# Half of the ktile pairs of the second MLP products by seven block products in place of eight

## The chip, the cores and the metric

The kernel runs on one core of one Trainium2 chip. The metric is the device time of one launch in microseconds (us). Engines are named as the profile names them: PE is TensorE, DVE is VectorE, ACT is ScalarE, POOL is GpSimd, and SP issues DMAs. PEld is TensorE's loading of stationary tiles.

## The reference

A trunk of two layers on an input of 256 tokens by 2048, in float32. Each layer has a mixer (layer 0: compressed, selected and window attention beside a low-rank one; layer 1: three dilated attentions) and an MLP with a hidden width of 8192:

```
def sq_relu_mlp(h, w1, w2):
    return jnp.square(jax.nn.relu(h @ w1)) @ w2
...
    for layer in range(DEPTH):
        u = rms_norm(h, g_mix_pre)
        m = even_mixer(u, *even_mix) if layer % 2 == 0 else odd_mixer(u, *odd_mix)
        h = h + rms_norm(m, g_mix_post)
        f = sq_relu_mlp(rms_norm(h, g_ffn_pre), *ffns[layer])
        h = h + rms_norm(f, g_ffn_post)
```

The change is in the product with `w2` (8192 by 2048), the second product of the MLP.

## The kernel before

All large products have float32 accuracy out of a reduced matmul format: each operand is split into a high part (`hi`, a rounded copy that ACT writes, `split` in L242 or, with a gain, L245) and a low part (`lo`, the remainder, that DVE writes, L243 or L246). A product is three matmuls: hi by hi, hi by lo, lo by hi. So each weight tile of 128 rows (a "ktile") by 1024 columns, which a 1 MB DMA brings as half of a `raw` tile, costs ACT and DVE one instruction each before PE can use it.

`weights` loads `raw` tiles from a pool of three buffers of their own (`wraw`), and splits them into `whi` and `wlo`, five buffers each. `job` runs a product with the tokens on the output's partitions; `job_T` runs one with the output transposed. A job takes all its ktiles one after another; each of the eight PSUM banks holds one output block, and when the last ktile is done the blocks are evacuated.

The MLP (`mlp`) walks the hidden width in four blocks of 2048 (`FBLK`). Per block:
- ff1, two halves of 1024 hidden columns (in the first block the first half is split in two jobs of 512): `job_T` leaves eight banks, four pairs of them. `done` adds the two parts of a bank (ACT copy L398, DVE add L399); `relu2` squares (ACT L628, L629); `hT.put` splits the result into the stationary tiles `hT` (ACT L242, DVE L243). The banks of the last two ktiles finish one after another.
- ff2, two halves of 1024 output columns: `job` over 16 ktiles, four blocks of 512 columns (2 token tiles by 2 column tiles): 12 matmuls of 512 columns per ktile. The result is copied to (first block, ACT) or added to (later blocks, DVE, L672) the sum `m` in SBUF.

The code is written job after job; the order of each engine's queue is set when the program is built. A load and a split stand as far forward in the queues as their buffers allow, so with pools of their own the first weights of the next job are split ahead of the evacuation of the one that runs. Each engine works through its queue in that order.

The pool `big` (tag "A", 11 buffers of 8 KB per partition) holds `uT`, `hT` (four buffers each), `m`, and the attention's tiles. `s2` is a pool of six scratch tiles of 512 columns. `h`, the residual, has a buffer of its own.

Of the kernel before, what the change touches and what calls it, by code (L numbers as in the profile page):

```python
# [18 lines left out]
P = 128  # L19
# [18 lines left out]
NA, NW = 11, 5  # L38
# [43 lines left out]
def trunk(ctx: ExitStack, tc: tile.TileContext, a: dict, out: bass.AP):  # L82
# [3 lines left out]
    wraw = ctx.enter_context(tc.tile_pool(name="wraw", bufs=3))  # L86
# [86 lines left out]
    h = cst.tile([P, T, D], F, name="h")  # L173
# [122 lines left out]
    def weights(W, k0, nk, cols, gT=None, g0=0, apart=False):  # L296
# [3 lines left out]
        for i in range(0, nk, m0):  # L300
            raw = wraw.tile([P, 2, 1024], F, name="raw")
# [166 lines left out]

    def chunks512(c0, n=1024):
# [101 lines left out]
    class PostNorm:  # L571


        def __init__(self, gname, eps=None):
            self.m = [A([P, D], F, "m") for _ in range(T)]
# [15 lines left out]
        def finish(self, t, then):  # L591
# [28 lines left out]
    def mlp(uT, w1, w2, gT, g0, ss, gname, then):  # L620
# [4 lines left out]
        pn = None  # L625
# [6 lines left out]
        def ff1(b, hT):  # L632
# [19 lines left out]
        eps = []  # L652
        for b in range(nb):
            hT = Split("hT", nk)
            ff1(b, hT)
            if b == 0:
# [5 lines left out]
                pn = PostNorm(gname, eps)  # L662
            end = b == nb - 1
# [554 lines left out]
```

## Time and profile before

| what | us |
|---|---|
| median of 3 runs | 2281.84 (2281.67 to 2282.22) |
| the profiled execution | 2280.53 |
| its span | 2278.6 |
| PE busy | 2255.6 |
| DVE busy | 1346.2 |
| ACT busy | 1250.0 |
| ff2, one half of one block (there are 16) | 87.2 |
| ff1, one half of one block | 88.9 |

The profiled execution has about 1.9 us outside its span. The MLP of layer 0 stands at 348.8 to 1061.7 us of the span, that of layer 1 at 1556.6 to 2267.0 us.

### The profile page before, as it was taken

The numbers are of one execution on the slowest core, as the hardware profiler recorded it, in microseconds if no ns is written. First come the engines' busy times: TensorE is split into PE (matmuls) and PEld (weight loads), VectorE is DVE, ScalarE is ACT, GpSimd is POOL, SyncE is SP. The second block draws the span as 40 slices with busy tenths as digits, with TensorE's granted clock in tenths as the row PEclk, the third lists the DMA queues.
The fourth block names the chain that finished last, engine by engine and source line by source line (L and its number), as shares of the span: only waits on it lengthen the run. The fifth ranks groups of instructions, "written<-read, shape, count | busy, mean of one in ns | idle before, by whom it ended". The sixth has DMA issues, their size and how long they took to land.

```text
span 2278.6 us, 30208 instructions
## 1 busy us (share of the span) xinstructions
PE 2255.6 (99%) x11949; PEld 1937.5 (85%) x11949; DVE 1346.2 (59%) x2059; ACT 1250.0 (55%) x1940; POOL 51.9 (2%) x44
## 2 busy tenths in 40 slices
PE   9999999999999999999999999999999999999997
PEld 9889887888888888887888888887888888888886
DVE  5877547544654554566565677847554554554555
ACT  5766547544644544555556666657554554554553
POOL 0000010000000000011000000001000000000002
PEclk9999999999999999999999999999999999999999
DMA  7844455565465555554554554555565555555553
GB/s 249 247 148 139 140 174 166 198 208 186 168 220 185 185 203 185 185 198 160 188 193 149 184 174 159 178 174 163 192 212 188 188 198 189 186 198 190 185 202 112
DMA packets 131177, 418.58 MB, mean 184 GB/s; under 512 B 6870, under 2 KB 7644, under 8 KB 130524
## 3 DMA queue, kind: packets, MB, share of 16 engines
q1 hardware_dynamic: 131036, 416.66, 54.3%
q8 instruction: 93, 1.52, 0.3%
q14 instruction: 48, 0.39, 0.1%
HBM read 414.54 MB, written 2.10 MB: 183 GB/s over the span
## 4 chain that ended last, share of the span: by engine, by line
PE 90%; issue 5%; DVE 2%; POOL 1%; ACT 1%; DMA 0%; DVEq 0%; POOLq 0%; SPq 0%; ACTq 0%
PE mm L361 27%; PE mm L405 19%; PE mm L409 10%; PE sb L361 6%; PE tb L361 6%; PE tb L405 4%; PE sb L405 4%; PE sb L409 2%; PE tb L409 2%; PE mm L435 2%; PE sb L539 2%; PE mm L443 2%; PE tb L283 1%; DVE h L603 1%; POOL m L589 1%
## 5 line engine op out<-in xcount | busy, mean ns | idle before, releaser
L246 DVE SCALAR_TENSOR_TENSOR wlo<-raw,gT,whi 128x512 fp32r<-128x512 f32 (+4 forms) x621 | 606.6, 1010 | 433.5 <-PE tb L409 208.2
L245 ACT ACTIVATE whi<-raw,gT 128x512 fp32r<-128x512 f32 (+4 forms) x621 | 551.2, 928 | 452.3 <-PE tb L405 238.0
L243 DVE TENSOR_TENSOR wlo<-raw,whi 128x1024 fp32r<-128x1024 f32 x304 | 376.6, 1245 | 356.8 <-ACT whi L242 356.8
L242 ACT ACTIVATE whi<-raw 128x1024 fp32r<-128x1024 f32 x304 | 320.7, 1061 | 384.5 <-PE mm L361 212.3
L405 PE MATMUL mm<-uT,whi 128*128 128x512 f32 x1952 | 503.5, 394 | 0.3 <-ACT z L845 0.3
L405 PEld LDWEIGHTS mm<-uT,whi 128*128 128x128 f32 x1952 | 346.9, 189 | 58.4 <-DVE s L399 0.7
L409 PEld LDWEIGHTS mm<-uT,wlo 128*128 128x128 f32 x1952 | 271.2, 190 | 22.3
L409 PE MATMUL mm<-uT,wlo 128*128 128x256 f32 x1952 | 280.3, 283 | 0.0
L361 PE MATMUL mm<-whi,hT 128*128 128x512 f32 x1024 | 280.3, 389 | 0.0
L361 PEld LDWEIGHTS mm<-whi,hT 128*128 128x128 f32 x1024 | 192.3, 188 | 39.7
L361 PE MATMUL mm<-whi,uT 128*128 128x512 f32 (+1 forms) x640 | 197.0, 398 | 0.0
L361 PE MATMUL mm<-wlo,hT 128*128 128x512 f32 x512 | 162.9, 389 | 0.0
L361 PE MATMUL tb<-whi,hT 128*128 128x512 f32 x512 | 160.6, 390 | 0.0
L361 PE MATMUL sb<-whi,hT 128*128 128x512 f32 x512 | 160.3, 389 | 0.0
L361 PEld LDWEIGHTS mm<-whi,uT 128*128 128x128 f32 x640 | 116.0, 189 | 19.9 <-ACT uT L242 0.2
L405 PE MATMUL tb<-uT,whi 128*128 128x512 f32 x448 | 122.8, 390 | 0.0
L405 PE MATMUL sb<-uT,whi 128*128 128x512 f32 x448 | 122.4, 390 | 0.0
L361 PEld LDWEIGHTS sb<-whi,hT 128*128 128x128 f32 x512 | 96.1, 188 | 20.0
L361 PEld LDWEIGHTS tb<-whi,hT 128*128 128x128 f32 x512 | 96.0, 188 | 19.8
L361 PEld LDWEIGHTS mm<-wlo,hT 128*128 128x128 f32 x512 | 96.2, 188 | 19.6
L361 PE MATMUL mm<-wlo,uT 128*128 128x512 f32 x320 | 104.9, 385 | 0.3 <-DVE wlo L246 0.3
L405 PEld LDWEIGHTS sb<-uT,whi 128*128 128x128 f32 x448 | 82.1, 188 | 15.3
(269 smaller groups left out, 2516.9 us busy)
## 6 DMA issues: line engine op xcount, KB each, us to landing
raw<-in_l_w_ff_dram SPq DMA_DIRECT2D x256, 1024.0 KB, 5.0
raw<-in_l_w_in_dram SPq DMA_DIRECT2D x87, 1024.0 KB, 5.1
raw<-in_l_w_out_dram SPq DMA_DIRECT2D x24, 1024.0 KB, 5.0
raw<-in_l_w_in_dram SPq DMA_DIRECT2D x8, 832.0 KB, 4.7
raw<-in_l_w_in_dram SPq DMA_DIRECT2D x8, 536.0 KB, 4.2
raw<-in_l_mla_w_uq_dram SPq DMA_DIRECT2D x4, 768.0 KB, 4.5
h<-in_x_dram SPq DMA_DIRECT2D x8, 256.0 KB, 5.8
raw<-in_l_mla_w_ukv_dram SPq DMA_DIRECT2D x2, 1024.0 KB, 5.0
```

The costliest lines, as they stand in the source:

```text
L242: nc.scalar.activation(hi, src, AF.Copy)
L243: eng.tensor_tensor(lo, src, hi.bitcast(F), ALU.subtract)
L245: nc.scalar.activation(hi, src, AF.Copy, scale=scale)
L246: nc.vector.scalar_tensor_tensor(lo, src, scale, hi.bitcast(F), ALU.mult, ALU.subtract)
L283: nc.tensor.transpose(pv[:, i, :], src[:, i * P:(i + 1) * P], ident)
L361: nc.tensor.matmul(ps[t, c][:, 0:w], xs, ws[:, offs[c]:offs[c] + w], start=(k == 0 and p == 0), stop=(k == nk - 1 and p == 2))
L405: nc.tensor.matmul(ps[b], wt[0][:, fs], mov.both(k), start=(k == 0), stop=False, skip_group_check=True)
L409: nc.tensor.matmul(ps[b][:, 0:SEQ], wt[1][:, fs], mov.at(k)[0], start=False, stop=(k == nk - 1), skip_group_check=True)
L435: nc.tensor.matmul(ps[b][:, f * SEQ:(f + 1) * SEQ], ws[:, fs], xs, start=(k == 0 and p == 0 and f == 0), stop=(k == nk - 1 and p == 2 and ...
L443: nc.tensor.matmul(ps[b][:, at:at + w], xs[:, tsl(t)], part(ws), start=(k == 0 and p == 0 and i == 0), stop=(k == nk - 1 and p == 2 and i ...
L539: nc.tensor.matmul(ps[:, parts[t]], q[:, tsl(t)], k[:, 0:(t + 1) * P], start=(i == 0), stop=(i == len(terms) - 1))
L589: eng.tensor_tensor(self.m[t][:, s], self.m[t][:, s], self.g[:, s], ALU.mult)
```

## The change

In ff2, half of the ktile pairs (four of the eight of a block) are computed by seven products of blocks in place of eight. A pair of ktiles gives, for two token tiles, a 2 by 2 product of blocks (two token tiles by two ktiles, times two ktiles by two column tiles): eight block products of three matmuls each, 24 in all. With seven products (`SEVEN`) of sums of blocks it is 21. The sums of the hidden values (`Sevens.put`) are built when ff1's second half of a block is evacuated; the sums of the weights (`wsum`) and their splits (`wboth`) when the weights come (`seven_weights`). `job_7` runs plain and seven pairs in turn (0, 4, 1, 5, 2, 6, 3, 7). It serves both column halves of the first three blocks and the first half of the fourth; the second half of the fourth goes by `job` as before.

The sums of products (`c11` to `p7`, eight banks) are no longer added into `m` in SBUF: `to_acc` copies a bank by ACT into an `s2` tile, which a DMA issued by POOL writes to DRAM (first block) or adds to it there (second and third block). `combine` loads and combines them during the fourth block, and `into` adds the fourth block's.

Buffers change as well. `wraw` is gone: `raw` tiles come from the tag "A", as do `wsum`, `wboth` and the tiles of `sums`; "A" has 16 buffers in place of 11. `h` is two tiles of "A", kept in DRAM during the MLP's later blocks and loaded again. `whi` and `wlo` share one tag of 10 buffers.

```diff
--- before.py
+++ after.py
-NA, NW = 11, 5
+NA, NW = 16, 10
...
-    wraw = ctx.enter_context(tc.tile_pool(name="wraw", bufs=3))
+    dram = ctx.enter_context(tc.tile_pool(name="dram", bufs=1, space=bass.MemoryType.DRAM))
...
+    def W4(name):
+        return whl.tile([P, 1024], R, name=name, tag="W")
...
-    h = cst.tile([P, T, D], F, name="h")
+    h = [A([P, D], F, f"h{t}") for t in range(T)]
...
-            raw = wraw.tile([P, 2, 1024], F, name="raw")
+            raw = A([P, 2, 1024], F, "raw")
...
-                        his = whl.tile([P, 1024], R, name="whi")
-                        los = whl.tile([P, 1024], R, name="wlo")
+                        his = W4("whi")
+                        los = W4("wlo")
...
+    class Sevens:
+        def __init__(self, stat, pairs):
+            self.stat, self.pairs = stat, pairs
+            self.tiles = [A([P, 2, 2, 512], R, "sums") for _ in range((len(pairs) + 1) // 2)]
...
+        def put(self, pair, y):
+            f = s2()
+            base = y[:, 0:P]
+            two = bass.AP(tensor=base.tensor, offset=base.offset, ap=[base.ap[0], [3 * P, 2], [1, P]])
+            nc.vector.tensor_tensor(
+                f[:, 0:2 * P].rearrange("p (i q) -> p i q", i=2),
+                y[:, P:2 * P].unsqueeze(1).to_broadcast([P, 2, P]), two, ALU.subtract)
+            nc.vector.tensor_tensor(f[:, 2 * P:3 * P], y[:, 0:P], f[:, P:2 * P], ALU.subtract)
+            nc.vector.tensor_tensor(f[:, 3 * P:4 * P], y[:, 2 * P:3 * P], f[:, 2 * P:3 * P], ALU.subtract)
+            i = self.pairs.index(pair)
+            split(self.tiles[i // 2][:, i % 2, 0, :], self.tiles[i // 2][:, i % 2, 1, :], f)
...
+    SUMS = ("s3", "s1", "s2", "s4")
+    def seven_weights(W, k0, c0, order, sevens):
+        for pair in order:
...
+            raw = A([P, 2, 1024], F, "raw")
+            r0 = (k0 + 2 * pair) * P
+            nc.sync.dma_start(raw, W[r0:r0 + 2 * P, c0:c0 + 1024].rearrange("(k p) c -> p k c", p=P))
+            parts = {}
+            def part(src, names, hi, lo):
+                split(hi, lo, src)
+                for i, name in enumerate(names):
+                    parts[name] = hi[:, i * 512:i * 512 + 512], lo[:, i * 512:i * 512 + 512]
+            if pair not in sevens.pairs:
...
+            sums = A([P, 4, 512], F, "wsum")
+            flat = raw.rearrange("p k c -> p (k c)")
+            b11, b12, b21, b22 = (flat[:, i * 512:i * 512 + 512] for i in range(4))
+            outer = bass.AP(tensor=b11.tensor, offset=b11.offset, ap=[b11.ap[0], [1536, 2], [1, 512]])
+            nc.vector.tensor_tensor(sums[:, 0:2, :], outer, b12.unsqueeze(1).to_broadcast([P, 2, 512]), ALU.add)
+            nc.vector.tensor_tensor(b12, sums[:, 0, :], b22, ALU.add)
+            nc.vector.tensor_tensor(sums[:, 2, :], b12, b21, ALU.add)
+            for src, names in (
+                    (raw[:, 1, :], [(1, 0), (1, 1)]), (raw[:, 0, :], [(0, 0), "t2"]),
+                    (sums[:, 0:2, :].rearrange("p i c -> p (i c)"), ["t1", "t3"])):
+                both = A([P, 2, 1024], R, "wboth")
+                part(src, names, both[:, 0, :], both[:, 1, :])
+            part(sums[:, 2, :], ["t4"], W4("whi")[:, 0:512], W4("wlo")[:, 0:512])
+            yield parts
...
+    SEVEN = (("c11", (0, 1), (1, 0)), ("c12", "s4", (1, 1)), ("p1", (0, 0), (0, 0)), ("p6", "s2", "t2"),
+             ("p5", "s1", "t1"), ("p7", "s3", "t3"), ("c21", (1, 1), "t4"))
+    LAST_SEVEN = tuple(SEVEN[i] for i in (0, 1, 6, 2, 4, 3, 5))
...
+        for j, pair in enumerate(order):
+            parts = next(gen)
+            seq = seq_of(pair)
+            for i, (b, which, form) in enumerate(seq):
+                xh, xl = sevens.at(pair, which)
+                wh, wl = parts[form]
+                first = b not in ps
+                if first:
+                    ps[b] = (mm_bank if b[0] == "c" else s_bank if b in ("p1", "p6") else t_bank)()
+                for p, (xs, ws) in enumerate(((xh, wh), (xh, wl), (xl, wh))):
+                    nc.tensor.matmul(ps[b], xs, ws, start=first and p == 0, stop=last[b] == (j, i) and p == 2,
+                                     skip_group_check=True)
+                bt.tick(3 * 512 / 2400)
+                if last[b] == (j, i):
+                    evac(b, ps[b])
...
+        order = [p for i in range(nk // 4) for p in (i, nk // 4 + i)]
+        BANKS = ("c11", "c12", "c21", "c22", "p1", "p5", "p6", "p7")
+        acc = [{b: dram.tile([P, 512], F, name=f"acc{c}{b}", tag=f"{gname}{c}{b}") for b in BANKS} for c in range(2)]
+        kept = [dram.tile([P, D], F, name=f"kept{t}", tag=f"{gname}kept{t}") for t in range(T)]
...
+                    if k // 2 in sevens.pairs:
+                        sevens.put(k // 2, y)
...
+        def ff2(b, sevens, c, evac):
+            job_7(sevens, w2, b * nk, c * 1024, order, evac)
+        def to_acc(b, c):
+            def f(name, ps):
+                y = s2()
+                nc.scalar.activation(y, ps, AF.Copy)
+                if b == 0:
+                    nc.gpsimd.dma_start(acc[c][name], y)
+                else:
+                    nc.gpsimd.dma_start(acc[c][name], y, accum_op=ALU.add)
+            return f
...
+        def combine(m, c):
+            pt = A([P, 4, 512], F, "pt")
+            p = {}
+            for i, name in enumerate(BANKS[4:]):
+                p[name] = pt[:, i, :]
+                nc.sync.dma_start(p[name], acc[c][name])
+            for t in range(T):
+                for n in range(2):
+                    nc.sync.dma_start(out_of(m, c, t, n), acc[c][f"c{t + 1}{n + 1}"])
+            for _ in range(4):
...
+            for dst, x, y, op in (
+                    (p["p6"], p["p6"], p["p1"], ALU.subtract), (o(0, 0), o(0, 0), p["p1"], ALU.add),
+                    (p["p5"], p["p5"], p["p6"], ALU.add), (o(0, 1), o(0, 1), p["p5"], ALU.add),
+                    (o(1, 1), o(1, 1), p["p5"], ALU.add), (o(1, 1), o(1, 1), p["p7"], ALU.add),
+                    (p["p6"], p["p6"], p["p7"], ALU.add), (o(1, 0), o(1, 0), p["p6"], ALU.subtract)):
+                add(dst, x, y, op)
+                yield
...
+                got[name] = y = s2()
+                nc.scalar.activation(y, ps, AF.Copy)
+                o = lambda t, n: out_of(m, c, t, n)
+                def add(dst, y, op=ALU.add):
+                    nc.vector.tensor_tensor(dst, dst, y, op)
+                if name[0] == "c":
+                    add(o(int(name[1]) - 1, int(name[2]) - 1), y)
+                elif name == "p1":
+                    add(o(0, 0), y)
...
-            def evac(base):
-                def f(t, c, ps):
-                    cc = base + c
-                    m = pn.m[t][:, cc * 512:(cc + 1) * 512]
-                    if b == 0:
-                        nc.scalar.activation(m, ps, AF.Copy)
-                    else:
-                        nc.vector.tensor_tensor(m, ps, m, ALU.add)
-                    if end:
-                        pn.chunk_done(t, cc)
-                return f
-            job(hT, w2, b * nk, nk, chunks512(0), evac(0))
-            job(hT, w2, b * nk, nk, chunks512(1024), evac(2), last=4 if end else 1, bank=all_banks(4),
-                after=(lambda t: pn.finish(t, then)) if end else None)
...
+            sevens = Sevens(hT, tuple(range(nk // 4, nk // 2)))
+            end = b == nb - 1
+            if end:
+                m = [A([P, D], F, "m") for _ in range(T)]
+                for c in range(2):
+                    bt.add(combine(m, c))
...
+                    nc.gpsimd.dma_start(kept[t], h[t])
+                    h[t] = None
+            if not end:
+                for c in range(2):
+                    ff2(b, sevens, c, to_acc(b, c))
+                continue
+            bt.flush()
+            pn = PostNorm(gname, eps, m)
+            for t in range(T):
+                h[t] = A([P, D], F, f"h{t}")
+                nc.sync.dma_start(h[t], kept[t])
+            ff2(b, sevens, 0, into(pn, 0, m))
+            def evac(t, c, ps):
+                o = m[t][:, 1024 + c * 512:1536 + c * 512]
+                nc.vector.tensor_tensor(o, ps, o, ALU.add)
+                pn.chunk_done(t, 2 + c)
+            job(hT, w2, b * nk, nk, chunks512(1024), evac, last=4, after=lambda t: pn.finish(t, then))
```

The change also moves instructions. The first place is the end of ff1 and the start of ff2 in the first block of layer 0, on ACT (`mm`, `sb`, `tb` are ff1's banks, `s2` the scratch tile of a pair of banks, `whi` the new weights). Before:

```order
L242 ACTIVATE whi_4431<-raw_4429 128x1024 [waits DMAHW4_49,DVE_49,PE_49]
L242 ACTIVATE whi_4451<-raw_4429 128x1024 [waits DVE_49,PE_49]
L242 ACTIVATE whi_4469<-raw_4467 128x1024 [waits DMAHW5_49,DVE_49,PE_49]
L398 ACTIVATE s2_4331<-mm_4015 128x256 [waits PE_49]
L398 ACTIVATE s2_4331<-mm_4016 128x256 [waits PE_49]
L398 ACTIVATE s2_4348<-mm_4017 128x256 [waits PE_49]
L398 ACTIVATE s2_4348<-mm_4018 128x256 [waits PE_49]
L628 ACTIVATE s2_4331<-s2_4331 128x512 [waits DVE_49]
L398 ACTIVATE s2_4365<-sb_4019 128x256 [waits PE_49]
```

After, the last rows of ff1's evacuation and the first of ff2's weights:

```order
L401 ACTIVATE s2_4420<-tb_4041 128x256 [waits PE_49]
L401 ACTIVATE s2_4420<-tb_4042 128x256 [waits PE_49]
L245 ACTIVATE sums_3619<-s2_4410 128x512 [waits DVE_49]
L733 ACTIVATE s2_4420<-s2_4420 128x512 [waits DVE_49]
L734 ACTIVATE s2_4420<-s2_4420 128x512 [waits Activation_49]
L245 ACTIVATE hT_3617<-s2_4420 128x2x256 [waits Activation_49]
L245 ACTIVATE sums_3619<-s2_4433 128x512 [waits DVE_49]
L245 ACTIVATE whi_4471<-raw_4469 128x1024 [waits DMAHW4_49]
L245 ACTIVATE whi_4475<-raw_4469 128x1024
```

Before, three weight tiles of ff2 (`whi_4431`, `whi_4451`, `whi_4469`) stand ahead of the first copy of a bank; now the first (`whi_4471`) stands behind the last row of the whole evacuation.

The same place on PE, the last matmuls of ff1 and the first of ff2. Before:

```order
L409 MATMUL tb_4022<-uT_3530,wlo_4320 128x256
L409 MATMUL tb_4022<-uT_3530,wlo_4324 128x256
L361 MATMUL mm_4435<-whi_4431,hT_3596 128x512 [waits DVE_49]
L361 MATMUL mm_4435<-wlo_4432,hT_3596 128x512
L361 MATMUL mm_4435<-whi_4431,hT_3596 128x512
L361 MATMUL mm_4439<-whi_4431,hT_3596 128x512 [waits DVE_49]
```

After:

```order
L412 MATMUL tb_4042<-uT_3530,wlo_4340 128x256
L412 MATMUL tb_4042<-uT_3530,wlo_4344 128x256
L564 MATMUL mm_4479<-whi_4471,hT_3614 128x512 [waits DVE_49,Activation_49]
L564 MATMUL mm_4483<-whi_4471,hT_3614 128x512 [waits DVE_49]
L564 MATMUL mm_4479<-wlo_4472,hT_3614 128x512 [waits DVE_49]
L564 MATMUL mm_4479<-whi_4471,hT_3614 128x512
L564 MATMUL mm_4483<-wlo_4472,hT_3614 128x512
```

PE's own order has not changed: ff2's first matmul follows ff1's last at once. It now waits for ACT and DVE, whose rows are those above.

The second place is the border between the two halves of ff1 in the second block of layer 0, on ACT. Before, weights of the next half and then the first copies of banks:

```order
L245 ACTIVATE whi_5301<-raw_5295,gT_942 128x1024
L245 ACTIVATE whi_5383<-raw_5381,gT_942 128x1024
L245 ACTIVATE whi_5387<-raw_5381,gT_942 128x1024
L245 ACTIVATE whi_5425<-raw_5423,gT_942 128x1024
L398 ACTIVATE s2_5309<-mm_4993 128x256
L398 ACTIVATE s2_5309<-mm_4994 128x256
L398 ACTIVATE s2_5326<-mm_4995 128x256
L398 ACTIVATE s2_5326<-mm_4996 128x256
```

After, the last rows of the evacuation and then the weights of the next half:

```order
L401 ACTIVATE s2_5498<-tb_5138 128x256
L734 ACTIVATE s2_5481<-s2_5481 128x512
L733 ACTIVATE s2_5498<-s2_5498 128x512
L245 ACTIVATE hT_5126<-s2_5481 128x2x256
L734 ACTIVATE s2_5498<-s2_5498 128x512
L245 ACTIVATE hT_5126<-s2_5498 128x2x256
L248 ACTIVATE whi_5521<-raw_5519,gT_942 128x1024
L248 ACTIVATE whi_5525<-raw_5519,gT_942 128x1024
```

Three weight tiles stood ahead of the first copy (L398); now none does: the first (`whi_5521`) follows the last split of `hT`.

The third place is the end of an ff2 half, on ACT. Before, in the first block, from the first half to the second (`m` is the sum in SBUF):

```order
L242 ACTIVATE whi_4711<-raw_4709 128x1024 [waits DMAHW5_49,DVE_49,PE_49]
L242 ACTIVATE whi_4731<-raw_4709 128x1024 [waits DVE_49,PE_49]
L242 ACTIVATE whi_4749<-raw_4747 128x1024 [waits DMAHW6_49,DVE_49,PE_49]
L242 ACTIVATE whi_4765<-raw_4747 128x1024 [waits DVE_49,PE_49]
L670 ACTIVATE m_4423<-mm_4435 128x512 [waits PE_49]
L670 ACTIVATE m_4423<-mm_4439 128x512 [waits PE_49]
L670 ACTIVATE m_4424<-mm_4443 128x512 [waits PE_49]
L670 ACTIVATE m_4424<-mm_4447 128x512 [waits PE_49]
L242 ACTIVATE whi_4783<-raw_4781 128x1024 [waits DMAHW7_49,DVE_49]
```

After, at the end of the second half of the first block, before ff1 of the next (`s2` goes to DRAM from here):

```order
L767 ACTIVATE s2_5086<-mm_4807 128x512
L767 ACTIVATE s2_5092<-mm_4811 128x512
L767 ACTIVATE s2_5098<-mm_4815 128x512
L767 ACTIVATE s2_5104<-sb_4860 128x512
L767 ACTIVATE s2_5110<-tb_4868 128x512
L767 ACTIVATE s2_5116<-sb_4864 128x512
L767 ACTIVATE s2_5122<-tb_4872 128x512
L248 ACTIVATE whi_5141<-raw_5139,gT_942 128x1024
L248 ACTIVATE whi_5145<-raw_5139,gT_942 128x1024
```

Before, four weight tiles of the next half (`whi_4711` to `whi_4765`) stand ahead of the evacuation, which is four copies; now all copies of the eight banks (the last seven are shown) stand ahead of the next job's first weights (`whi_5141`).

## Rows read from the trace of the kernel before

**Rows 1.** The page: span, busy time by engine, granted TensorE clock in 40 slices.

```profile
span 2278.6 us, 30208 instructions
...
PE 2255.6 (99%) x11949; PEld 1937.5 (85%) x11949; DVE 1346.2 (59%) x2059; ACT 1250.0 (55%) x1940; POOL 51.9 (2%) x44
...
PEclk9999999999999999999999999999999999999999
```

**Rows 2.** Windows: half a second-product block, then an ff1 half.

```profile
core 0: us, PE busy (x) PEld busy (x) DVE busy (x) ACT busy (x) POOL busy (x), PEclk, DMA share, GB/s
443.40:530.65 87.25, 87.25 (x387) 72.29 (x386) 44.28 (x40) 43.49 (x52) 0.00 (x0) 1.00 0.60 206
530.65:619.56 88.91, 88.91 (x514) 78.28 (x512) 45.69 (x48) 46.69 (x61) 0.00 (x0) 1.00 0.56 189
```

**Rows 3.** Timeline of TensorE at 619.56 us: ff1 ends, second product begins.

```profile
start us, us, engine line op out<-in xcount [idle before <-releaser]
...
619.33 0.40 PE L409 MATMUL tb<-uT,wlo 128*128 128x256 f32 x2
619.56 0.40 PE L361 MATMUL mm<-whi,hT 128*128 128x512 f32 x1
```

**Rows 4.** Timeline of ScalarE (ACT) around the same 619.56 us.

```profile
612.04 2.01 ACT L242 ACTIVATE whi<-raw 128x1024 fp32r<-128x1024 f32 x2 [3.47 <-PE tb L405]
614.88 0.39 ACT L398 ACTIVATE s<-mm 128x256 f32<-128x256 f32 x1 [0.83 <-PE mm L409]
...
621.95 0.65 ACT L629 ACTIVATE s<-s 128x512 f32<-128x512 f32 x1
622.47 1.08 ACT L242 ACTIVATE whi<-raw 128x1024 fp32r<-128x1024 f32 x1
```

**Rows 5.** Groups of ScalarE instructions by line and shape: busy us, mean ns.

```profile
L245 ACT ACTIVATE whi<-raw,gT 128x1024 fp32r<-128x1024 f32 x291 | 325.5, 1146 | 336.7 <-PE tb L405 238.0 <-PE tb L361 46.1 <-PE mm L361 17.1
L242 ACT ACTIVATE whi<-raw 128x1024 fp32r<-128x1024 f32 x304 | 320.7, 1061 | 384.5 <-PE mm L361 212.3 <-PE tb L361 134.3 <-PE tb L405 27.7
...
L398 ACT ACTIVATE s<-mm 128x256 f32<-128x256 f32 x122 | 46.7, 382 | 60.6 <-PE mm L409 60.2
...
L628 ACT ACTIVATE s<-s 128x512 f32<-128x512 f32 x60 | 38.0, 634 | 1.9 <-DVE s L399 1.9
L242 ACT ACTIVATE hT<-s 128x512 fp32r<-128x512 f32 x60 | 38.0, 633 | 0.0
...
L614 ACT ACTIVATE m<-mm 128x512 f32<-128x512 f32 x16 | 9.3, 591 | 5.5 <-PE mm L361 5.5
```

**Rows 6.** Groups of VectorE (DVE) instructions by line and shape.

```profile
L243 DVE TENSOR_TENSOR wlo<-raw,whi 128x1024 fp32r<-128x1024 f32 x304 | 376.6, 1245 | 356.8 <-ACT whi L242 356.8
L246 DVE SCALAR_TENSOR_TENSOR wlo<-raw,gT,whi 128x1024 fp32r<-128x1024 f32 x291 | 366.5, 1281 | 330.0 <-PE tb L409 208.2 <-ACT whi L245 96.7 <-ACT whi L242 24.7
...
L399 DVE TENSOR_TENSOR s<-mm,s 128x256 f32<-128x256 f32 x122 | 47.9, 417 | 8.8 <-ACT s L398 8.3
L243 DVE TENSOR_TENSOR hT<-s,hT 128x512 fp32r<-128x512 f32 x60 | 41.3, 688 | 17.2 <-ACT hT L242 15.9
...
L1102 DVE TENSOR_SCALAR o_acc<-o_acc,ca 128x128 f32<-128x128 f32 x32 | 8.1, 278 | 0.0
```

**Rows 7.** The page, DMA issues: count, KB each, median us to landing.

```profile
raw<-in_l_w_ff_dram SPq DMA_DIRECT2D x256, 1024.0 KB, 5.0
...
out_dram<-h SPq DMA_DIRECT2D x8, 256.0 KB, 2.6
```

**Rows 8.** Windows around the last matmul, columns as in Rows 2.

```profile
2265.00:2267.00 2.00, 1.96 (x9) 1.31 (x7) 2.00 (x3) 0.03 (x1) 1.76 (x1) 1.00 0.53 201
...
2269.00:2270.00 1.00, 0.00 (x0) 0.00 (x0) 0.94 (x3) 0.59 (x2) 0.14 (x1) 0.74 0.72 252
2270.00:2272.00 2.00, 0.00 (x0) 0.00 (x0) 1.56 (x3) 0.72 (x1) 1.17 (x2) 0.50 0.00 0
```

**Rows 9.** Timeline of TensorE: the eight warm-up matmuls at the start.

```profile
1.19 3.59 PE L205 MATMUL tb<-warm 128*128 128x512 bf16 x8 [1.19 <-DVE warm L166]
```

More of the change, by code (lines that the diff above doesn't have):

```diff
@@ L467, in job_T, with at @@
                 evac_tok(b - npr, ps[b])
+    class Sevens:
[13 more added lines that the diff above has]
+            split(self.tiles[i // 2][:, i % 2, 0, :], self.tiles[i // 2][:, i % 2, 1, :], f)
+        def at(self, pair, which):
+            if which in SUMS:
+                i, q = self.pairs.index(pair), tsl(SUMS.index(which))
+                v = self.tiles[i // 2][:, i % 2, :, q]
+                return v[:, 0, :], v[:, 1, :]
+            t, k = which
+            return self.stat.at(2 * pair + k, t)
@@ new lines, in trunk @@
+    SUMS = ("s3", "s1", "s2", "s4")
[10 more added lines that the diff above has]
+            if pair not in sevens.pairs:
+                for k in range(2):
+                    part(raw[:, k, :], [(k, 0), (k, 1)], W4("whi"), W4("wlo"))
+                yield parts
[13 more added lines that the diff above has]
+            part(sums[:, 2, :], ["t4"], W4("whi")[:, 0:512], W4("wlo")[:, 0:512])
+            yield parts
@@ new lines, in trunk, with job_7, seq_of @@
+    SEVEN = (("c11", (0, 1), (1, 0)), ("c12", "s4", (1, 1)), ("p1", (0, 0), (0, 0)), ("p6", "s2", "t2"),
+             ("p5", "s1", "t1"), ("p7", "s3", "t3"), ("c21", (1, 1), "t4"))
+    LAST_SEVEN = tuple(SEVEN[i] for i in (0, 1, 6, 2, 4, 3, 5))
+    def job_7(sevens, W, k0, c0, order, evac):
+        gen = seven_weights(W, k0, c0, order, sevens)
+        ps = {}
+        def seq_of(pair):
+            if pair in sevens.pairs:
+                return LAST_SEVEN if pair == order[-1] else SEVEN
+            return tuple((f"c{t + 1}{n + 1}", (t, k), (k, n)) for k in range(2) for t in range(T) for n in range(2))
+        last = {}
+        for j, pair in enumerate(order):
+            for i, (b, _, _) in enumerate(seq_of(pair)):
+                last[b] = (j, i)
+        for j, pair in enumerate(order):
+            parts = next(gen)
[12 more added lines that the diff above has]
+                    evac(b, ps[b])
@@ L630, in relu2, with ff1 @@
             return y
-        def ff1(b, hT):
+        def ff1(b, hT, sevens):
             def evac(t, c, ps):
@@ new lines, in out_of @@
+        def out_of(m, c, t, n):
+            return m[t][:, c * 1024 + n * 512:c * 1024 + n * 512 + 512]
+        def combine(m, c):
[10 more added lines that the diff above has]
+            o = lambda t, n: out_of(m, c, t, n)
+            add = nc.vector.tensor_tensor
+            for dst, x, y, op in (
[4 more added lines that the diff above has]
+                add(dst, x, y, op)
+                yield
@@ L778, in compress @@
         for i in range(2):
-            raw = wraw.tile([P, 2, 1024], F, name="raw")
+            raw = A([P, 2, 1024], F, "raw")
             nc.sync.dma_start(raw.rearrange("p k (l e) -> p (k l) e", e=HD), w1v[:, 16 * i:16 * i + 16, :])
```

48 lines of the change are left out of this document (33 added, 15 removed).

## The prediction

> **What bounds the kernel now.** I read the page first: PE is busy 2255.6 of a span of 2278.6 us, at full granted clock in every slice but for its ends, and no other engine is above 60% [rows 1]. So a matmul taken away is worth its whole time, as long as nothing holds PE. Then the windows by stage: half a block of the second product is 87.25 us with no PE gap in it, an ff1 half 88.91 us [rows 2]. Then the border of two jobs: ff1's last matmul pair starts at 619.33, the second product's first matmul at 619.56, one pitch later [rows 3]. ACT shows why there is no gap: it split two weight tiles of the coming job at 612.04, before the first copy of a finished bank at 614.88, and put the next one at 622.47 between the steps of the evacuation [rows 4]. The profile says that PE never waits because ACT and DVE always hold a few weight tiles ready, about 2.7 us of PE each.
>
> **What it removes.** 386 weight loads, one per matmul, stand in the 87.25 us: 0.226 us per matmul [rows 2]. A seven pair has 21 matmuls in place of 24. Per MLP four pairs in seven half blocks (three blocks times two halves, and one), 28; in both MLPs 56. 56 x 3 x 0.226 = 38.0 us. The additions into `m` that go away were on DVE, which is not the bound: nothing.
>
> **What it adds on ACT and DVE inside the second product.** A seven pair costs DVE four 1024-wide operations and three 512-wide ones, 4 x 1.245 + 3 x 0.69 = 7.0 us, a plain one two, 2.5 us [rows 6]; together 9.5 us against (24 + 21) x 0.226 = 10.2 us of PE. ACT has 5 x 1.06 + 0.63 = 5.9 us [rows 5]. Both fit, but only while PE's wait doesn't come from elsewhere.
>
> **What it moves, the decisive part.** With `raw` in the shared tag "A", loads and splits of the next job stand behind the last evacuation of the job before, on ACT and on DVE, as the pieces of the order show. Of 62 job starts some 45 now have their first weight split behind one of the last ten matmuls of the previous job; before, all were 50 matmuls or more ahead. The load itself lands in 5.0 us [rows 7] and is issued in time; the split is what is late. Let T be the end of the previous job on PE. I walk the queues by hand with the durations of [rows 5, 6]; a row that follows another on ACT without a wait starts some 0.1 us before that one's shown end (0.65 us shown at 621.95, the next row 0.52 us later [rows 4]).
>
> *ff1 to the second product, 8 times.* A bank ends with two matmuls of 512 columns (0.45 us) and two of 256 (0.23 us [rows 3]), so the four pairs of banks finish 1.36 us apart, the last at T. Each goes copy, DVE add, two ACT steps, split: 0.38 + 0.42 + 3 x 0.634 = 2.7 us, so the first ends at T - 1.4. In the new queue the split of the sums stands between one pair's copies and its first ACT step, and it waits for DVE (split of `hT` 0.69, a sum 0.28). This makes the period of a pair 3.64 us: hT of the last pair at T + 9.5, sums at T + 11.1, first weights on ACT at T + 12.1, on DVE at T + 13.35. PE has two matmuls that need only the high part (0.45 us): it stands 12.9 us. 8 x 12.9 = 103 us. From below, ACT's own rows alone (8 copies and 16 others at pitch, 10.5 us from T - 4.1) give 8.2 us; from above, every step in series with DVE's gives 18 us: 66 to 145 us.
>
> *Between the halves of ff1, 8 times.* No sums here, so ACT's rows go on almost without a wait: 8 x 0.27 + 12 x 0.52 = 8.4 us from T - 4.1, to T + 4.4; two weight tiles with gain (1.15 and 1.0) to T + 6.5; PE has one matmul before it needs the second tile: 6.3 us, in the first block (only four banks' worth of queue ahead) 5.0. 6 x 6.3 + 2 x 5.0 = 48 us; 34 to 60 for 1.5 us either way.
>
> *Into and out of the second half of the second product.* Only the last bank's copy is in the way (0.59, as the copy of [rows 5]): weights at T + 1.9, low part at T + 3.1, less 0.45: 2.65 us, 8 times; into the next ff1 2.75 us, 6 times: 38 us.
>
> *The other late starts, 20.* Projections, the attention's jobs, the first ff1 of an MLP: from 1.9 us (one copy and a 512-wide split) to 6.3 us (as between the ff1 halves) each, 38 to 126 us. Most have one tile to evacuate, so I take 3.55 us each: 71 us.
>
> *Weights of a seven pair inside a job.* Their load waits for a buffer that PE frees 40 matmuls, 9.0 us, ahead of use; load, sums and first split need 5.0 + 1.13 + 1.25 = 7.4 us. A little slack in the steady run, late by about 2.1 us once in each first half, 17 us; 0 if the load is quick, 38 us if all 42 inner ones are 0.9 us late.
>
> *The accumulating DMAs.* Eight evacuations share six `s2` tiles, so the seventh and eighth copy wait until the first two DMAs have landed; there are about 4.2 us for that. The trace shows no accumulating DMA; the nearest row, 256 KB to DRAM, lands in 2.6 us [rows 7], which is hidden: 0. From above, a landing of 8 us (three times the row) holds 14 halves by 4 us: 56 us. I take 0. The Trainium skill ("DMA: Bandwidth & Descriptors", Anatomy of one DMA, SWDGE path) gives a fixed 2 us and a rate for DMAs that POOL issues; an estimate by it is 2.6 us too, and it says nothing of what the addition costs.
>
> *TensorE's clock.* The last matmul ends within 0.05 us of 2267.0; the granted clock is 1.00 until then, 0.74 on average from 2269.0 to 2270.0, and 0.50 after [rows 8]: it fell to the level of 1.2 GHz about 2.5 us after PE went idle. At the start eight matmuls took 3.59 us, 0.449 each, twice the 0.226 of later [rows 9]: 1.8 us lost. About 27 of the gaps above are well over 2.5 us (8 + 8 in the MLP, 11 elsewhere). At 1.8 us each 49 us; 0 if PE would wait for weights then anyway, 97 us if the low level lasts twice as long. The Trainium skill ("TensorE: Matmul & The Clock Gate", HAM oscillation) says that PE gaps inside a kernel send the clock down each time and that every burst then starts cold; the end of this trace agrees for one gap (1.00 to 0.50), a gap inside the kernel this trace does not have.
>
> *Small.* Keeping and reloading `h` and the 16 loads of `combine` are DMAs beside ff1 at a DMA share of 0.56 to 0.60 [rows 2]; the additions are on DVE, half idle there: 0, at most some 5 us each MLP if they delay a weight split.
>
> **The sum.** -38 + 103 + 48 + 38 + 71 + 17 + 49 = +288 us. On the profiled execution's 2280.5 us that is 2568.5; the median of the runs shown is 1.3 above that execution, so 2570 us. The lower ends together (66, 34, 38, 38, 0, 0) give +138, the upper ones +422; these don't all fall together.
>
> **Rivals.**
> 1. *Not slower: the evacuation is quick enough.* If ACT and DVE, idle for over 40% [rows 1], ran the last evacuation and the first splits within what PE has queued, only the 38 us would show: 2244 us. The point from which it decides is 38.0/62 = 0.6 us of stall per job start. Against it: the shortest chain, one copy and one split, is longer than that [rows 5], and there is no matmul of another job to fill it. 3%.
> 2. *Stalls without the clock.* The lower clock falls into stretches in which PE waits for weights anyhow: 2521 us. 22%.
> 3. *The clock stays low longer after each gap*, as the rule of the clock page taken at its worst: 97 us in place of 49, 2618 us. For it: [rows 8] shows how soon it falls. 15%.
> 4. *The accumulating DMAs hold the `s2` tiles*: 2626 us. For it: only six tiles; against it: 2.6 us in [rows 7]. 12%.
> 5. *A shorter chain*: DVE and ACT overlap the pairs as if the sums didn't interpose, 8.2 us at ff1's end, the other starts at 1.9 us, and no clock: -38 + 66 + 48 + 38 + 38 + 17 = +169, 2451 us. 13%.
> 6. *It doesn't do what it says*: banks or buffers make seven pairs run no shorter than eight; the 38 us are missing, 2608 us. 3%, and it moves the sum little.
>
> The forecast has 32%. All cases but the first are slower. 2440 to 2660 us holds some 8 in 10. A change of over 0.2%, 4.6 us, is what a measurement of this kernel can tell: faster 3%, within that 1%, slower 96%.
>
> **What would show it.** In the profile after: PE busy lower by some 38 us, or more if the clock is full, while the span is longer; PE idle, with ACT's or DVE's weight splits as its releaser, of about 13 us at each first matmul of the second product and 6 between ff1's halves; in ACT's timeline the first split after the last sum. The windows after such gaps should show a granted clock below 1.00. The 0.226 us per matmul should be found in the seven pairs. Wrong would be: no PE idle at those borders (rival 1); gaps inside the seven pairs larger than those at the borders (DVE or the loads are the bound); the last copies of a half waiting for a DMA (rival 4).

## The result: 2670 us, 17% slower

| | us |
|---|---|
| before, median | 2281.76 |
| after, median of 4 (2666.24 to 2676.87) | 2670.43 |
| ratio | 1.1705 (95% interval 1.1679 to 1.1732) |
| forecast (range) | 2570 (2440 to 2660) |

The direction and the place were as forecast; the time lies 10 us above the range. The page of the changed kernel, its parts 1, 2 and 6, against [rows 1] and [rows 7]:

```profile
span 2671.6 us, 30876 instructions
...
PE 2346.2 (88%) x11781; PEld 1976.3 (74%) x11781; DVE 1645.4 (62%) x2483; ACT 1407.3 (53%) x2180; POOL 125.5 (5%) x144
...
PEclk9999999889898899988999999999898899899988
...
raw<-in_l_w_ff_dram SPq DMA_DIRECT2D x256, 1024.0 KB, 7.2
...
acc0c<-s POOLq DMA_DIRECT2D x24, 256.0 KB, 7.1
acc0p<-s POOLq DMA_DIRECT2D x24, 256.0 KB, 6.8
acc1c<-s POOLq DMA_DIRECT2D x24, 256.0 KB, 7.9
acc1p<-s POOLq DMA_DIRECT2D x24, 256.0 KB, 11.7
```

The 168 matmuls fewer are there (11949 to 11781). PE is busy 90.6 us longer all the same, where the prediction looked for some 38 us less: work at a low clock counts as busy time too. It is busy for 88% in place of 99% of the span. By median the DMAs to DRAM land in 7 to 12 us, not in the 2.6 us of [rows 7].

What PE waits for (engine and line that waits, what it waits for, us in total, times, longest):

```profile
PE mm L564 <- ACT whi L245: 142.9, 18, 12.0
PE mm L408 <- ACT whi L248: 104.7, 24, 8.5
PE mm L364 <- ACT whi L245: 18.3, 6, 4.0
```

Three rows hold 266 us: all but 9 us of it is the first weight split of a job on ACT, as predicted (the 9 us lie inside the second product). The end of ff1, where [rows 3] had no gap. PE:

```profile
485.81 0.40 PE L412 MATMUL tb<-uT,wlo 128*128 128x256 f32 x2
498.22 1.22 PE L564 MATMUL mm<-whi,hT 128*128 128x512 f32 x2 [12.01 <-ACT whi L245]
499.48 0.80 PE L564 MATMUL mm<-wlo,hT 128*128 128x512 f32 x1
```

ACT at the same place, against [rows 4]:

```profile
484.80 0.64 ACT L401 ACTIVATE s<-mm 128x256 f32<-128x256 f32 x2
485.85 0.63 ACT L245 ACTIVATE sums<-s 128x512 fp32r<-128x512 f32 x1 [0.41 <-DVE s L488]
...
488.38 0.64 ACT L401 ACTIVATE s<-sb 128x256 f32<-128x256 f32 x2
...
491.96 0.64 ACT L401 ACTIVATE s<-tb 128x256 f32<-128x256 f32 x2
...
496.59 0.63 ACT L245 ACTIVATE sums<-s 128x512 fp32r<-128x512 f32 x1 [0.96 <-DVE s L488]
497.12 1.99 ACT L245 ACTIVATE whi<-raw 128x1024 fp32r<-128x1024 f32 x2
```

The pairs of banks follow one another every 3.58 us (484.80, 488.38, 491.96; the prediction's walk of the queues had 3.64), the sums of the last one end at 497.2, 11.0 us after PE's last matmul (11.1 in the walk), and the weights come right behind. They did not come late from DRAM. SP, from 440 to 500 us:

```profile
447.63 5.93 SPq L508 DMA_DIRECT2D raw<-in_l_w_ff_dram  x2
```

These two loads landed within 5.0 us, by 458 us; ACT splits the first of them at 497.12. Only the split is behind the evacuation, not the load. The matmuls after such a gap run at the low level. Windows before, in and after the gap (columns as in [rows 2]):

```profile
480.00:486.20 6.20, 6.20 (x38) 5.29 (x36) 2.75 (x8) 3.56 (x8) 0.00 (x0) 1.00 0.00 0
486.20:498.20 12.00, 0.00 (x1) 0.00 (x0) 8.95 (x22) 9.91 (x19) 0.00 (x0) 0.71 0.00 0
498.20:504.80 6.60, 6.54 (x15) 4.67 (x16) 6.17 (x7) 3.19 (x4) 0.00 (x0) 0.50 0.45 159
504.80:520.00 15.20, 15.20 (x69) 12.57 (x68) 13.62 (x14) 8.59 (x10) 0.00 (x0) 1.00 0.40 141
```

The granted clock falls in the gap, stays at 0.50 for 6.6 us of work, and is 1.00 again.

The end of a first half of the second product, block two, on ACT:

```profile
754.97 0.60 ACT L767 ACTIVATE s<-tb 128x512 f32<-128x512 f32 x1
758.46 0.60 ACT L767 ACTIVATE s<-sb 128x512 f32<-128x512 f32 x1 [2.88 <-DMA acc0c<-s]
759.81 0.60 ACT L767 ACTIVATE s<-tb 128x512 f32<-128x512 f32 x1 [0.76 <-DMA acc0c<-s]
760.31 1.99 ACT L245 ACTIVATE whi<-raw 128x1024 fp32r<-128x1024 f32 x2
```

The seventh and eighth copy wait 2.88 and 0.76 us for DMAs that still hold `s2` tiles, and the next job's weights stand behind them: PE has been idle since 754.4, for 7.0 us, where 2.65 us were forecast. Copies that wait for a DMA were the prediction's own sign of its rival 4.

**Where the 393 us of span went**, by the idle time of PE between matmuls and the busy time under a granted clock of 0.5:

| term | forecast | measured |
|---|---|---|
| 168 matmuls fewer | -38 | -38 |
| ff1 to second product, 8 | 103 | 96 |
| between ff1 halves, 8 | 48 | 44 |
| into and out of a second half, 14 | 38 | 99 |
| other late starts and small gaps | 71 | 53 |
| inside the second product | 17 | 9 |
| clock (by the record) | 49 | 110 |
| left over | | 20 |

PE's idle time rose from 11.4 to 312.7 us. It is busy for 221 us at the clock of 0.5, in 44 stretches; if at full clock all of it took half, 110 us are lost. That is an upper figure, since some of those 221 us are waits for weights (see the runs with matmuls in the gaps). The 9 us inside the second product all lie in the fourth block, not in every block as forecast. Of the 20 us left over, 18 are in PE's busy time. Some 12 of them are, by an estimate, the ends of matmuls: a matmul is shown for 0.39 us but the next one starts after 0.23 us, so the last one ahead of a gap shows 0.16 us more, and there are 70 gaps more than before. The rest is not explained.

### The profile page after: what moved, and what is told of

The parts are those of the page before. It is cut to its first block, busy times and chain, and to the rows that moved or that the text cites. A ratio compares the mean times of both kernels' runs of the same rounds, so it can differ in the third digit from the quotient of the medians.

```text
span 2671.6 us, 30876 instructions
## 1 busy us (share of the span) xinstructions
PE 2346.2 (88%) x11781; PEld 1976.3 (74%) x11781; DVE 1645.4 (62%) x2483; ACT 1407.3 (53%) x2180; POOL 125.5 (5%) x144
## 4 chain that ended last, share of the span: by engine, by line
PE 46%; issue 37%; ACT 5%; DVE 5%; DMA 3%; POOL 3%; SPq 0%; POOLq 0%; DVEq 0%; ACTq 0%
PE mm L408 12%; PE mm L364 12%; PE mm L412 6%; PE mm L564 3%; DMA raw<-in_l_w_ff_dram 2%; PE mm L438 2%; PE sb L408 2%; PE tb L408 2%; PE mm L446 1%; PE sb L640 1%; PE sb L412 1%; PE tb L412 1%; DMA acc1c<-s 1%; ACT whi L248 1%; PE tb L286 1%
## 5 line engine op out<-in xcount | busy, mean ns | idle before, releaser
L408 PE MATMUL mm<-uT,whi 128*128 128x512 f32 x1952 | 534.8, 412 | 105.4 <-ACT whi L248 104.7
L408 PEld LDWEIGHTS mm<-uT,whi 128*128 128x128 f32 x1952 | 362.3, 198 | 179.8 <-ACT whi L248 118.6
L564 PE MATMUL mm<-whi,hT 128*128 128x512 f32 x1008 | 351.3, 420 | 142.9 <-ACT whi L245 142.9
L246 DVE TENSOR_TENSOR wlo<-raw,whi 128x1024 fp32r<-128x1024 f32 x192 | 233.0, 1250 | 152.0 <-ACT whi L245 151.9
L245 ACT ACTIVATE wboth<-raw 128x1024 fp32r<-128x1024 f32 x112 | 118.6, 1059 | 258.8 <-DVE raw L525 128.0
L245 ACT ACTIVATE whi<-raw 128x1024 fp32r<-128x1024 f32 x192 | 193.4, 1049 | 88.3 <-PE mm L364 63.1
L564 PE MATMUL mm<-wlo,hT 128*128 128x512 f32 x504 | 211.9, 420 | 0.4
L246 DVE TENSOR_TENSOR wboth<-raw,wboth 128x1024 fp32r<-128x1024 f32 x112 | 136.9, 1222 | 25.1 <-ACT wboth L245 25.1
L402 DVE TENSOR_TENSOR s<-mm,s 128x256 f32<-128x256 f32 x122 | 50.8, 422 | 163.6 <-ACT s L401 163.4
L401 ACT ACTIVATE s<-mm 128x256 f32<-128x256 f32 x122 | 45.5, 381 | 187.1 <-PE mm L412 186.7
L364 PEld LDWEIGHTS mm<-whi,uT 128*128 128x128 f32 x640 | 121.3, 196 | 27.3 <-ACT whi L248 4.9
## 6 DMA issues: line engine op xcount, KB each, us to landing
acc1p<-s POOLq DMA_DIRECT2D x24, 256.0 KB, 11.7
```

Source lines behind the costliest of these rows:

```text
L245: nc.scalar.activation(hi, src, AF.Copy)
L246: eng.tensor_tensor(lo, src, hi.bitcast(F), ALU.subtract)
L364: nc.tensor.matmul(ps[t, c][:, 0:w], xs, ws[:, offs[c]:offs[c] + w], start=(k == 0 and p == 0), stop=(k == nk - 1 and p == 2))
L401: nc.scalar.activation(y, ps[b][:, SEQ:2 * SEQ], AF.Copy)
L402: nc.vector.tensor_tensor(y, ps[b][:, 0:SEQ], y, ALU.add)
L408: nc.tensor.matmul(ps[b], wt[0][:, fs], mov.both(k), start=(k == 0), stop=False, skip_group_check=True)
```

## The experiments

Times are medians; the ratio is to the kernel before in the same runs.

**The shared tag alone, in the kernel before.**

```diff
-NA, NW = 11, 5
+NA, NW = 14, 5
...
-    wraw = ctx.enter_context(tc.tile_pool(name="wraw", bufs=3))
...
-            raw = wraw.tile([P, 2, 1024], F, name="raw")
+            raw = A([P, 2, 1024], F, "raw")
```

> The kernel before with one thing changed: the raw tiles come from the tag A (14 buffers in place of 11 and a pool of 3); no sevens, no sums, no DMAs to DRAM. Theory (the shared tag puts the first weight split of a job behind the last evacuation, and this alone makes most of the stalls): PE idle of about 6 us at each start of the second product (8) and between the ff1 halves (8), 45 us at the other late starts, and 27 or so falls of the clock at 2 to 2.6 us each: about 2480 us. Rival (the sums and the DMAs to DRAM make the stalls): 2282 us, as before, within 10.

2508.41 us, ratio 1.0994 (1.0972 to 1.1016). PE's waits:

```profile
PE mm L404 <- ACT whi L244: 58.5, 17, 5.9
PE mm L360 <- ACT whi L241: 56.5, 12, 5.8
```

With no seven product and no DMA to DRAM in it, taking `raw` from "A" costs 227 us: 5.76 us at each start of the second product, 5.85 us between ff1's halves (4.39 in the first block), and a clock of 0.5 over 133 us of work. The rival falls. It also separates the sums: at ff1's end they make 12.0 us out of 5.8, 50 us in eight places. It took 28 us more than expected.

**A pool of its own for raw again, in the changed kernel.**

```diff
-NA, NW = 16, 10
+NA, NW = 13, 10
...
+    wraw = ctx.enter_context(tc.tile_pool(name="wraw", bufs=3))
...
-            raw = A([P, 2, 1024], F, "raw")
+            raw = wraw.tile([P, 2, 1024], F, name="raw")
```

> The changed kernel with one thing undone: raw tiles have a pool of three buffers of their own again, tag A has 13 buffers in place of 16. Theory (shared tag): the first weights stand 41 matmuls or more ahead of their job again, PE idle at the job borders goes, the clock stays up, and the 38 us saved show: 2244 us, up to 2275 if 13 buffers make the weights of a seven pair late. Rival (sums in the evacuation and the accumulating DMAs stall PE by themselves): 2500 us or more.

2368.08 us, ratio 1.0387 (1.0369 to 1.0406). 302 of the 389 us go with this one edit, and the gaps at the job borders with them. But it is 86 us slower than before, not 38 faster, and outside both of the expected cases. PE's idle time is still 74 us above the kernel before, and 59 us of work run at the clock of 0.5. What PE waits for now:

```profile
PE mm L565 <- ACT wboth L246: 35.0, 8, 6.6
PE sb L409 <- ACT s L768: 7.4, 4, 2.5
```

ACT at the end of ff1 shows the first of them (PE is idle from 451.55):

```profile
451.85 0.64 ACT L402 ACTIVATE s<-tb 128x256 f32<-128x256 f32 x2
452.90 0.63 ACT L246 ACTIVATE sums<-s 128x512 fp32r<-128x512 f32 x1 [0.41 <-DVE s L489]
453.57 0.63 ACT L734 ACTIVATE s<-s 128x512 f32<-128x512 f32 x1
454.11 1.04 ACT L246 ACTIVATE wboth<-raw 128x1024 fp32r<-128x1024 f32 x1
```

The plain pair was split ahead, so PE starts without a gap; the weights of the first seven pair still stand in the queue behind the sums.

**14 buffers of A in place of 13 in that kernel** (and 8 tiles for plain weights).

```diff
-NA, NW = 13, 10
+NA, NW = 14, 8
```

> The changed kernel with a pool of three for raw tiles, as in the run with 13 buffers in tag A (2368 us), but 14 buffers in A, paid for by 8 in place of 10 tiles for plain weights. Theory (what is left there is the weights of a seven pair waiting for a buffer of A, 3.65 us at the first seven pair of a block and up to 1 us at others): these gaps fall by half or more: 2310 to 2340 us. Rival (they wait for ACT and DVE, which still have the evacuation with its sums in their queues): 2360 to 2380 us.

2370.60 us, ratio 1.0386 (1.0371 to 1.0402): no gain.

```profile
PE mm L565 <- ACT wboth L246: 40.1, 8, 7.2
```

The gap at the first seven pair is 4.28 us (3.65 with 13 buffers), not smaller. The rival holds: together with ACT's rows of the run with 13, where the split of `wboth` comes right behind the other rows without a wait for a buffer, it is the queue and not the buffer.

**Three seven pairs, and two plain pairs first.**

```diff
-        order = [p for i in range(nk // 4) for p in (i, nk // 4 + i)]
+        orders = [0, 1, 4, 2, 5, 3, 6, 7], [0, 1, 4, 2, 5, 3, 7, 6]
...
-            sevens = Sevens(hT, tuple(range(nk // 4, nk // 2)))
+            sevens = Sevens(hT, (4, 5, 6))
```

> As the run with 14 buffers, with three seven pairs in place of four in each block, two plain pairs at its start, and in the first three blocks a plain pair at its end. 42 seven pairs save 28.5 us in place of 38. If the evacuation ahead of the first seven pair holds its weights, two plain pairs (10.9 us of PE) cover it and the gap of 3.65 us goes, and the copies of the eight banks come in two groups, so that the DMAs to DRAM hold nothing: 2260 to 2290 us. If buffers are the cause, no better than the run with 14 buffers and four pairs plus 9.5 us.

2330.43 us, ratio 1.0213 (1.0196 to 1.023).

```profile
PE mm L565 <- ACT wboth L246: 7.4, 8, 1.9
```

The wait for `wboth` falls from 40.1 to 7.4 us in the same 8 places, as the queue theory says. The time doesn't reach the 2260 to 2290 us expected: PE's idle time is still 45 us above the kernel before and 45 us of work run at the clock of 0.5 (23 us lost), together more than the 28.5 us saved. No version that was run beats the kernel before.

**No accumulating DMAs.**

```diff
-                else:
-                    nc.gpsimd.dma_start(acc[c][name], y, accum_op=ALU.add)
```

> The changed kernel without the accumulating DMAs of the second and third block (their partial sums are left out of the result); the first block's plain writes to DRAM stay. Theory (s2 tiles held by accumulating DMAs make the borders into and out of a second half longer than the evacuation's chain): in blocks two and three the gaps of 7.0 and 8.3 us fall to 2.7 us, those of block one (4.9 and 6.3) stay; 8 gaps, 40 us, and up to 20 us of clock: 2610 to 2632 us. Rival (the chain of copies and splits is that long by itself): 2670 us, as the changed kernel.

2624.78 us, ratio 1.1496 (1.147 to 1.1522), 46 us less than the changed kernel. In blocks two and three the gaps of 6.7 to 8.5 us are 3.1 to 3.2 us; those of block one (4.8 and 6.3), with their plain writes, stay. As the theory has it. In the changed kernel itself the plain writes of block one (L769) and the accumulating ones (L771) can be set side by side (the landing lines are of all 32 and all 64):

```profile
L769 POOL DMA_DIRECT2D acc0c<-s x8: 542/542/547, 539.3 to 1957.5; - x8
...
DMA to landing us min/median/max: 2.6/5.8/8.4
L771 POOL DMA_DIRECT2D acc0c<-s x16: 860/878/1216, 750.6 to 2381.1; - x16
...
DMA to landing us min/median/max: 6.6/8.4/16.5
```

The first plain write at the end of a first half, with no other of these DMAs ahead of it, landed in 2.6 us, just as [rows 7] had it; the first accumulating one at the same place landed in 6.6 to 7.8 us. But the plain writes at the end of the second half took 6.4 to 8.4 us as well.

**Ten s2 tiles, at the price of one buffer of A.**

```diff
-NA, NW = 16, 10
+NA, NW = 15, 10
-    scr = ctx.enter_context(tc.tile_pool(name="scr", bufs=6))
+    scr = ctx.enter_context(tc.tile_pool(name="scr", bufs=10))
```

> The changed kernel (raw in the tag A) with ten s2 tiles in place of six and 15 buffers in A in place of 16: no copy of a bank need wait for a DMA. Theory (six s2 tiles, held by DMAs that land in 7 to 12 us): the gaps into and out of a second half fall from 4.8 to 8.5 us to about 2.7 us, 14 of them by 60 us in all, and the clock falls less often: 2590 to 2615 us. Rival (the DMAs themselves slow the loads, or DVE and ACT are late): above 2650 us.

2771.45 us, ratio 1.2146 (1.2126 to 1.2166), 101 us more than the changed kernel. The gaps out of the second half did fall to 3.2 us, but those into it stay at 3.9 to 4.8 us in the first three blocks, and new ones of 1.3 to 4.1 us, mostly of 3, stand at plain pairs inside the second product, two in most halves. ACT there:

```profile
512.11 0.61 ACT L245 ACTIVATE whi<-wsum 128x512 fp32r<-128x512 f32 x1
517.71 2.00 ACT L245 ACTIVATE whi<-raw 128x1024 fp32r<-128x1024 f32 x2 [4.99 <-DMA raw<-in_l_w_ff_dram]
520.28 1.06 ACT L245 ACTIVATE wboth<-raw 128x1024 fp32r<-128x1024 f32 x1 [0.57 <-DMA raw<-in_l_w_ff_dram]
```

ACT waits 5 us for a load. SP issued it only at 512.35, released by DVE's split of a `wboth`: it had waited for a buffer. In all ACT waits 192.5 us in 42 places to split a plain weight because its load is not there (`whi`), against 24.4 us in 8 places in the changed kernel. The run mixes two things, so it was made again:

**Ten s2 tiles, 16 buffers of A, 8 tiles for plain weights.**

```diff
-NA, NW = 16, 10
+NA, NW = 16, 8
-    scr = ctx.enter_context(tc.tile_pool(name="scr", bufs=6))
+    scr = ctx.enter_context(tc.tile_pool(name="scr", bufs=10))
```

> The changed kernel with ten s2 tiles in place of six, this time paid for by the tiles for plain weights (8 in place of 10), with all 16 buffers of tag A. Theory (the borders into and out of a second half are long because DMAs hold the six s2 tiles, and the loss with 15 buffers of A came from loads that waited for a buffer): the 14 gaps fall from 4.8 to 8.5 us to 1.4 to 3.2 us, the new gaps of 3 us inside the second product are not there: 2590 to 2620 us. Rival (ten s2 tiles by themselves let the DMAs crowd the loads): gaps of 3 us at the plain pairs again, above 2700 us.

2627.94 us, ratio 1.1515 (1.1495 to 1.1534), 42 us less than the changed kernel, where 50 to 80 were expected: 8 us above that range. The end of a first half in block two, on ACT, as shown for the changed kernel:

```profile
743.21 0.60 ACT L767 ACTIVATE s<-tb 128x512 f32<-128x512 f32 x1
743.69 0.62 ACT L767 ACTIVATE s<-sb 128x512 f32<-128x512 f32 x1
744.16 0.63 ACT L767 ACTIVATE s<-tb 128x512 f32<-128x512 f32 x1
744.64 2.04 ACT L245 ACTIVATE whi<-raw 128x1024 fp32r<-128x1024 f32 x2
```

The copies follow one another without a wait, the gap is 3.1 us (7.0 in the changed kernel), and no gaps of 3 us appear inside the first three blocks. The DMAs land no sooner (6.8 to 13.3 us by median): they are only not waited for.

**Matmuls in the gaps.** First 48 unread ones in each of six 12 us gaps:

```diff
+        def filler(n):
+            ps = mm_bank()
+            for _ in range(n):
+                nc.tensor.matmul(ps, uT.at(0)[0][:, 0:P], uT.both(0), start=True, stop=True)
...
+            if b < nb - 1 and c == 0:
+                filler(48)
```

> The changed kernel with 48 matmuls of 512 columns, whose result nobody reads, at the end of ff1 in blocks one to three of each MLP: they fill 10.9 of the 12.0 us in which PE stands there. Theory (the idle PE lets the clock fall, and the low clock costs about 3.3 us after each such gap): no low clock after these six gaps, about 20 us less: 2650 us. Rival (after the gap PE waits for weights anyhow, so the low clock costs nothing): 2670 us, as the changed kernel, or some us more.

2656.58 us, ratio 1.1635 (1.1616 to 1.1654), 13.9 us less, 2.3 us per gap. By the record it would be 20 us: work at 0.5 falls from 221 to 180 us. The windows of the first such gap, to be set beside those of the changed kernel:

```profile
486.80:499.00 12.20, 11.06 (x49) 8.82 (x49) 9.14 (x22) 10.12 (x19) 0.00 (x0) 1.00 0.00 0
499.00:505.60 6.60, 6.54 (x28) 5.07 (x29) 6.17 (x7) 3.20 (x4) 0.00 (x0) 1.00 0.46 159
```

The clock stays at 1.00, and the 6.6 us after the gap hold 28 matmuls in place of 15. Then 18 gaps:

```diff
...
+                if b > 0:
+                    filler(22 if c else 20 if b == 1 else 28)
```

> The changed kernel with unread matmuls in 18 of its long gaps: 48 at the end of ff1 (blocks one to three), 20 or 28 at the end of ff2 (blocks one to three), 22 between the ff1 halves (blocks two to four), each somewhat shorter than the gap. The gaps stay in the order of the work, only PE is busy in them. Theory (the fall of the clock costs 2.3 us per gap, as the six filled gaps gave 13.9 us): 18 x 2.3 = 41 us less, 2630 us, and the low stretches in the record fall by about 18 x 10 us. Rival (the low clock is mostly hidden behind late weights): 2650 us or more.

2643.16 us, ratio 1.1586 (1.1568 to 1.1603), 27.3 us less, where 41 were expected. Work at the clock of 0.5 falls from 221 to 137 us, by the record 42 us at full clock. Part of the difference is that the fillers are busy 133 us (572 matmuls) and take away only 123 us of idle time, so some 10 us of them stand past the gap. PE's busy time without the fillers fell by 15.5 us in the run with six and by 37 us in this one, against 20 and 42 by the record: the record counts a tenth to a quarter too much. By the runs' times the fall of the clock costs 1.5 to 2.3 us per gap, by the record 2.5; the runs of one kernel lie up to 11 us apart, so 1.5 and 2.3 can't be told from one another.

## Why the prediction was outside its range

- *The saving* (38 us): right in count, and small beside the rest.
- *The move of the first weight split* was the cause. The kernel before with the shared tag alone is 227 us slower; the changed kernel with raw in its own pool loses 302 of its 389 us.
- *The walk of the queues*: 12.9 us forecast, 12.0 measured at ff1's end; 6.3 and 5.0 against 5.85 and 4.39 between the halves. The other late starts were put at 71 us and are 53.
- *Failed: "The accumulating DMAs ... I take 0".* The price came from the one row of a 256 KB store, at the kernel's end, 2.6 us [rows 7]. At the end of a half, eight together, they land in 6.8 to 11.7 us (median by tile), against the 4.2 us of cover that the prediction worked out. The term into and out of a second half is 99 us in place of 38, 61 us more; the upper end in the prediction was 56. Of the 61, 40 us lie in blocks two and three, with accumulating DMAs, and 12 in block one, whose DMAs are plain writes. The other 10 are in the fourth block, which writes nothing to DRAM there: PE waits 4.0 us for ACT's first split and another 3.7 us for DVE's, in each layer. Leaving the accumulating DMAs out takes 46 us away, more `s2` tiles 42 us, each with the clock that goes with the gaps.
- *Mis-sized: "At 1.8 us each 49 us".* 44 low stretches in place of 27, since gaps of 3 to 5 us often bring the clock down too, and by the record each costs more than the 1.8 us of the warm-up matmuls [rows 9]. By the record 110 us, an upper figure; the runs with fillers show 1.5 to 2.3 us for each gap that they fill. The Trainium skill ("TensorE: Matmul & The Clock Gate", HAM oscillation) describes a kernel in which PE's waits send the clock down, so that each burst of matmuls starts at the low level. The trace agrees for the 12 us gaps: 0.50 after one and 1.00 with it filled. It is not so after every shorter gap: in the run with ten `s2` tiles and 16 buffers the clock is 1.00 in the 6.1 us after the gap of 3.2 us at 585.7.
- *The range.* Rivals 3 (longer low clock, +48 us) and 4 (DMAs hold `s2`, +56 us) stood as alternatives to one another. Rival 4 came true, and the clock cost about what rival 3 had, though by more falls and not by falls of twice the length. Costs like these add: 2570 + 48 + 56 = 2674 us. That this lies so near 2670 is partly luck, since four other terms came out some 37 us lower and 20 us are left over. The prediction's upper ends, added up, give +466 us, or +522 with the 56 of the DMAs, where it writes +422; with any of these the range would have reached the result.
- *Rival 1* had nothing for it. In the kernel with the tag undone PE still loses time in the second product: even with the order restored, the sums and the DMAs cost more than the 38 us, which the prediction had not asked.

Left open: the part of the 20 us that is not the ends of matmuls; and what makes the DMAs land late. The addition is part of it (2.6 us for the first plain write against 6.6 to 7.8 us at the same place), but plain writes land late too at the end of a second half, where the 16 DMA engines are busy throughout (586 to 601 us: share 1.02; at the end of the first half, 538 to 549 us: 0.78). How much is the loads beside them and how much the queue of POOL, no run separates. Nor does a run show how the build comes to put the splits behind the evacuation when the tag is shared, only that it does.

## What to carry to other kernels

A change of buffer tags can also change the order of the queues: here the splits of weights that had landed some 40 us earlier stood behind an evacuation. Before buffers are merged, look where the first instruction of the next job then stands in the queues of the engines that feed TensorE; a few microseconds there, at dozens of job starts, outweigh a saving of 168 matmuls. A price read off a transfer in a quiet stretch is a lower end, not a value. And causes that can hold together belong into the range as a sum, not as alternatives.

## What the runs showed of the hardware

- In the changed kernel a 256 KB write to DRAM that POOL issues landed in 2.6 to 8.4 us (median 5.8, 32 plain ones), one that adds to what is there in 6.6 to 16.5 us (median 8.4, 64 of them). A store from SP at the quiet end of the kernel before took 2.6 us [rows 7], and so did a plain write from POOL with none ahead of it.
- 1 MB weight loads of the MLP land in 7.2 us in the changed kernel and in 5.0 us before [rows 7]. With the shared tag alone they take 5.1 us, with the sevens and the DMAs to DRAM but a pool of their own 4.9 us, without the accumulating DMAs 6.9 us. So neither the tag nor the DMAs make it alone; why both together do is not shown.
- After a gap of 12 us PE did 15 matmuls in 6.6 us, and 28 with the gap filled; unread matmuls in a gap that cannot be removed gave back 13.9 us in six places.
